# New SBUF places for an up projection's operands, w_out's weights split earlier and kept in DRAM, and new step orders

## The chip, the cores and the metric

The kernel runs on one core of a Trainium2 chip. The time is the device time of one execution in microseconds; that of several runs is given as their median. The engines: PE is TensorE, ACT is ScalarE, DVE is VectorE, POOL is GpSimd, and SP is the engine that issues nearly all DMA transfers here, one after the other in the order of its program. Every engine works its instructions off in program order and waits on semaphores for what others make.

## The reference

One step of one layer of a decoder, for a prompt of 2048 rows and a sample group of 8 sequences with 8 new rows each. D is 1024, the inner width 4096.

```python
h = rmsnorm(x, g_pre_mix)
proj = h @ w_in                                   # 1024 x 1280: q (512), k (128), v (128), u (512)
attn = sliding-window attention with rotary q, k and a sink per head   # window 128, 8 heads, 2 kv heads
pooled = per group: (mean of the last 2/4/8/16 rows of u - u) @ pool_w, times pool_scale
mix = concat(rmsnorm(attn, g_attn), rmsnorm(pooled, g_pool)) @ w_out
x = x + rmsnorm(mix, g_post_mix)
hf = rmsnorm(x, g_pre_mlp)
ff = square(relu(hf @ w_up)) @ w_down
x = x + rmsnorm(ff, g_post_mlp)
x = x + sigmoid(x @ w_ple_gate + b_ple_gate) * (pe @ w_ple)
```

Beside the two y, the outputs are the last 128 rows of k and v and the last 15 of u of each group. For the sample group most of these rows are those of the input states, shifted by 8 places: they are copied from DRAM to DRAM.

## The kernel before

**Arithmetic.** A product of 32-bit numbers is made of three passes with rounded halves: the high half (fp32r) times the high half, high times low and low times high. So every operand is "split": ScalarE casts or scales it into the high half (`split_into`, L195 to L197; for weights with a gain `A.mul`), VectorE subtracts that from the whole and gets the low half (`lo_of`, L127; for weights with a gain `scalar_tensor_tensor`, STT below).

**First stage (0 to about 452 us).** The sample rows are tile -1, the prompt's 16 tiles of 128 rows are 0 to 15. For each tile `head` loads x, its transposed copy xt and the rotary table cs; `front` makes q, k, v and u (products qps, kvps, ups with the split w_in, wi); `attention`, `pooling` and `finish` follow one tile behind, and `finish` stores the tile's mix to DRAM (mixd, L633). w_in is loaded in eight slices through a ring of four buffers (`load_w_in`, L322 to L327). The work of a tile is woven by hand-written strings (ORDER, L44): each letter takes one step of `a` attention, `p` pooling, `f` the next tile's front, `l` the last tile's finish, `e` extra work; ORDER1 and ORDER2 serve the last two tiles. A scheduler then orders the instructions of each engine from that, and may take DMAs without waits much earlier: the three state copies of L1100 to L1102 stand in the text in the up projection, but in SP's program in sixth to eighth place.

**w_out (452 to about 633 us).** In the last tile, as `e`, the class `Mixed` loads w_out raw in 8 units of two 128-row pieces by 512 columns, scales and splits them (`unit`, L210 to L227), and starts w_out's products (`product`, L240; tile of PSUM: pab). mr is a tile's mix read back, ms its split. After each tile come residual, second norm, and transposed h, stored to DRAM with its sums (hfd). The prompt's last two tiles' residual and turning are "late": they run in the up projection.

**Up projection (633 to about 1296 us).** The product hf @ w_up goes by a 7-product scheme in place of 8: the rows stand in three blocks, the columns in 16 pairs (`DFF // 256`). One `UpQuad` is a block and a pair j: seven products of 12 matmuls of 128x352, in the order p1, p2, p6, p7, p5, and `end` in the next round. Their left operands are the weights' seven combinations (raw -> g, differences at L984), their right ones seven operands of the block (loaded from hfd as sp, split into op; `load_ops`). In the first round two quads run side by side. `rest` (after p6 of that round) turns the second late tile, adds four op places, and loads operands five and six. `Ring` is a list of buffers that are used in turn; a pool's buffers lie where earlier pools lay, and a load into one waits until their last reader is done.

**Down projection, gate and the end (1296 to 2188 us).** Neither changes but for the state copies.

## Time and profile before

| | us |
|---|---|
| runs | 2188.45, 2188.64, 2188.88 (median 2188.64) |
| the profiled execution, its own time | 2190.07 |
| its span in the profile | 2188.3 |
| busy: PE / DVE / ACT / POOL | 2135.2 / 1591.6 / 958.8 / 568.5 |
| waits of PE that the trace names, the five longest groups | 7.5, 7.1, 6.0, 5.5, 4.3 |

The busy times overlap; an engine that is idle costs nothing unless the end waits for it. In a list of waits a row reads: engine, the waiting line, the releasing engine with its tile and line, then microseconds in total, number, and the longest. In a table of stretches a row reads: stretch, its length, then for each engine busy microseconds with the number of instructions, the clock that TensorE was granted (1.00 is full), the DMA engines' mean busy share, and GB/s. In a timeline: start, duration, engine, line, operation, and in brackets the idle time ahead of it with what ended it. A matmul at half clock counts as busy, so lost clock does not show as idle time.

### The profile page before, as it was taken

The page shows a single profiled execution, that of the slowest core. Times are in us where ns is not written, and L with a number is a line of the kernel's source. Part 1 is how long each engine was busy: PE and PEld are TensorE (multiplying, and loading weights), DVE is VectorE, ACT ScalarE, POOL GpSimd, SP SyncE. Part 2 cuts the span into 40 slices and gives each one's busy share as a digit, 9 for nine tenths or more (in the row PEclk, how much of TensorE's full clock was granted, in tenths as well). Part 3 has the DMA queues.
Part 4 walks back from the last instruction along what each step waited for, and adds up shares of the span by engine and source line. Part 5 has one row for each costly group of instructions (what it writes and reads, how often), then busy time and mean ns, then how long its engine had stood idle before and what let it go on. Part 6 is the DMA issues. An engine that isn't in the chain of part 4 may idle for free. (4 is left out here: it accounts for less than half of the span.)

```text
span 2188.3 us, 31100 instructions
## 1 busy us (share of the span) xinstructions
PE 2135.2 (98%) x11435; PEld 1884.1 (86%) x11435; DVE 1591.6 (73%) x2716; ACT 958.8 (44%) x1856; POOL 568.5 (26%) x642
## 2 busy tenths in 40 slices
PE   7999999889989999999999999999999999999999
PEld 5888888678878999999999988788888888888887
DVE  5788889866587777655755565888988888876553
ACT  4666666644465445444644454332232233232221
POOL 2334333233341000000000035535535535300000
PEclk9999999989999999999999999999999999999999
DMA  6212212457799768766676642222222221342211
GB/s 224 67 61 84 68 61 73 136 173 216 214 278 326 234 216 261 224 194 192 201 221 192 195 125 68 89 72 76 89 80 77 90 94 63 118 136 82 87 54 39
DMA packets 305985, 303.64 MB, mean 139 GB/s; under 512 B 78950, under 2 KB 257330, under 8 KB 299657
## 3 DMA queue, kind: packets, MB, share of 16 engines
q1 hardware_dynamic: 305833, 301.66, 44.1%
q8 instruction: 90, 1.47, 0.3%
q14 instruction: 62, 0.51, 0.1%
HBM read 208.78 MB, written 94.12 MB: 138 GB/s over the span
## 5 line engine op out<-in xcount | busy, mean ns | idle before, releaser
L1020 PE MATMUL up<-op,g 128*128 128x352 f32 x1344 | 433.6, 324 | 8.3 <-ACT snap L1027 7.5
L1021 PE MATMUL up<-op,g 128*128 128x352 f32 x1344 | 432.9, 322 | 5.5 <-DVE op L127 5.5
L1022 PE MATMUL up<-op,g 128*128 128x352 f32 x1344 | 421.8, 324 | 2.2 <-DVE g L127 2.2
L1247 DVE TENSOR_TENSOR z<-dn,z 128x512 f32<-128x512 f32 x416 | 277.2, 684 | 72.4 <-PE dn L1239 64.3
L127 DVE TENSOR_TENSOR g<-raw,g 128x512 fp32r<-128x512 f32 x336 | 229.0, 700 | 86.2 <-ACT g L197 85.8
L1020 PEld LDWEIGHTS up<-op,g 128*128 128x128 f32 x1344 | 252.7, 188 | 10.2 <-ACT snap L1027 8.6
L1021 PEld LDWEIGHTS up<-op,g 128*128 128x128 f32 x1344 | 254.2, 189 | 6.3 <-DVE op L127 6.1
L1022 PEld LDWEIGHTS up<-op,g 128*128 128x128 f32 x1344 | 251.2, 189 | 2.7 <-DVE g L127 2.7
L197 ACT CAST g<-raw 128x512 fp32r<-128x512 f32 x336 | 203.9, 623 | 104.5 <-PE up L1022 90.0
L1186 POOL TENSOR_TENSOR raws<-raws 128x1024 f32<-128x1024 f32 x32 | 84.4, 2647 | 619.1 <-DVE wr L127 424.1
L1237 PE MATMUL dn<-wr,ms 128*128 128x512 f32 x512 | 199.3, 390 | 0.8 <-DVE z L1247 0.8
L1238 PE MATMUL dn<-wr,ms 128*128 128x512 f32 x512 | 199.2, 389 | 0.0
L1239 PE MATMUL dn<-wr,ms 128*128 128x512 f32 x512 | 198.2, 389 | 0.0
L1034 DVE TENSOR_TENSOR t<-up,snap 128x352 f32<-128x352 f32 x144 | 71.1, 521 | 116.0 <-ACT snap L1027 99.8
L1237 PE MATMUL dn<-wr,m 128*128 128x512 f32 x384 | 149.5, 389 | 1.7 <-DVE z L1247 1.7
L1238 PE MATMUL dn<-wr,m 128*128 128x512 f32 x384 | 149.4, 389 | 0.0
L1239 PE MATMUL dn<-wr,m 128*128 128x512 f32 x384 | 149.1, 389 | 0.0
L197 ACT CAST m<-fr 128x512 fp32r<-128x512 f32 (+1 forms) x128 | 65.2, 513 | 188.5 <-PE dn L1239 166.6
L830 POOL TENSOR_TENSOR s<-fr 128x256 f32<-128x256 f32 x64 | 53.8, 840 | 321.4 <-DVE ms L127 222.0
L1027 ACT COPY snap<-up 128x352 f32<-128x352 f32 x144 | 61.1, 454 | 168.9 <-PE up L1022 168.8
L197 ACT CAST wr<-raws 128x1024 fp32r<-128x1024 f32 x66 | 69.1, 1051 | 119.2 <-PE dn L1239 57.8
L1237 PEld LDWEIGHTS dn<-wr,ms 128*128 128x128 f32 x512 | 96.1, 188 | 21.3 <-issue 1.2
(269 smaller groups left out, 4943.4 us busy)
## 6 DMA issues: line engine op xcount, KB each, us to landing
raw<-in_w_up_dram SPq DMA_DIRECT2D x160, 256.0 KB, 4.6
raw<-upt SPq DMA_DIRECT2D x32, 1024.0 KB, 7.8
fr<-ffd SPq DMA_DIRECT2D x64, 512.0 KB, 3.7
ffd<-r SPq DMA_DIRECT2D x96, 256.0 KB, 2.7
upt<-raw SPq DMA_DIRECT2D x16, 1024.0 KB, 4.0
raws<-in_w_down_dram SPq DMA_DIRECT2D x32, 512.0 KB, 5.0
sp<-hfd SPq DMA_DIRECT2D x21, 704.0 KB, 7.3
x<-in_x_prompt_dram SPq DMA_DIRECT2D x16, 512.0 KB, 4.5
```

The source lines that it names most:

```text
L127: eng.tensor_tensor(out=out, in0=full, in1=hi.bitcast(F32), op=ALU.subtract)
L197: copy(out=dst[:, 0], in_=src)
L1020: T.matmul(ps, l[0], r[0], start=st, stop=False, skip_group_check=not fresh)
L1021: T.matmul(ps, l[0], r[1], start=False, stop=False, skip_group_check=not fresh)
L1022: T.matmul(ps, l[1], r[0], start=False, stop=c == 3, skip_group_check=not fresh)
L1027: A.copy(out=s, in_=ps)
L1034: V.tensor_tensor(out=t, in0=ps, in1=s, op=ALU.add)
L1186: G.tensor_tensor(out=t, in0=x, in1=y, op=ALU.subtract)
L1237: T.matmul(ps, l[0], r[0], start=fresh and j == 0, stop=False, skip_group_check=not fresh)
L1238: T.matmul(ps, l[0], r[1], start=False, stop=False, skip_group_check=not fresh)
L1239: T.matmul(ps, l[1], r[0], start=False, stop=j == 1, skip_group_check=not fresh)
L1247: V.tensor_tensor(out=z, in0=ps, in1=z, op=ALU.add)
```

## The change

- **Start.** `load_gains` comes first, then xt of tile -1 and two slices of w_in, only then x and cs; the ring has six buffers. The state copies now are issued through `queue` (which keeps program order) in the down projection.
- **w_out.** `split_w_out` is the `e` of tiles 3 to 10: one unit a tile, two pieces of 128x512 each loaded, scaled, subtracted and stored to a DRAM tensor wod, with two raw buffers (wraw) and one for the split pieces (wsp). `unit` then only loads 1 MB of finished halves. Tiles 3 to 10 have their own string, ORDERW; ORDER1 and ORDER2 are new.
- **Up projection.** Each operand has a named place; the rings for weights, raw weights and operands lie otherwise, so that some no longer lie over what w_out's last products read. The first round is one quad. The late residuals and turnings are spread over the first two rounds, and in the third `space` makes room for two more operands' places and three of g.

```diff
+ORDERW = "e a e f f l f f f f p a f f f e f a f f p a f f f f p a a l"
-ORDER1 = "f a f f f l f f a f f a f p f f f f p l f a a p a"
-ORDER2 = "e a p l a p e l a p e a e a e e"
+ORDER1 = "f a f f f l a f f f p f a f f f f f p l f a a a p"
+ORDER2 = "e a p l a a e l a p e a e p e e"
...
+    wod = {(u, nh): dp.tile([P, 2, 2, 512], F32, name=f"wod{u}{nh}") for u in range(4) for nh in range(2)}
...
         def unit(self, u, nh):
-            ns = slice(nh * 512, nh * 512 + 512)
-            raw = self.mrp.tile([P, 2, 512], F32, tag="raw", bufs=4, name="raw")
-            if u >= 2:
-                SY.dma_start(raw, w_out[u * 256 : (u + 1) * 256, ns].rearrange("(k p) f -> p k f", p=P))
-            else:
...
             w = self.wo[nh * 4 + u].tile([P, 2, 2, 512], F32R, name="wo")
-            for k in range(2):
-                g = gout[:, 2 * u + k : 2 * u + k + 1]
-                A.mul(out=w[:, 0, k], in_=raw[:, k], mul=g)
-                V.scalar_tensor_tensor(
-                    out=w[:, 1, k], in0=raw[:, k], scalar=g, in1=w[:, 0, k].bitcast(F32), op0=ALU.mult, op1=ALU.subtract
-                )
+            SY.dma_start(w.bitcast(F32), wod[u, nh])
             self.w[u, nh] = w
...
         def load_w_in(k):
-            raw = over.pool.tile([P, INC], F32, tag="raw", bufs=4, name="raw")
+            raw = over.pool.tile([P, INC], F32, tag="raw", bufs=6, name="raw")
...
+            if t < 0:
+                queue(xt[:, :, :n], x_t[:, :, c0 : c0 + n])
+                for k in range(2):
+                    load_w_in(k)
             x = fp.tile([P, D], F32, tag="x", bufs=1, name="x")
             queue(x[:n], xrows(t))
...
+        def split_w_out(u, nh):
+            ns = slice(nh * 512, nh * 512 + 512)
+            raws = []
+            for c in (2 * u, 2 * u + 1):
+                raw = over.pool.tile([P, 512], F32, tag="wraw", bufs=2, name="wraw")
+                raws.append(raw)
+                if u >= 2:
+                    SY.dma_start(raw, w_out[c * P : (c + 1) * P, ns])
+                else:
+                    for g in range(2):
+                        SY.dma_start(raw[g * HD : g * HD + HD], w_out[g * 256 + c * HD : g * 256 + (c + 1) * HD, ns])
+            yield
+            for k, raw in enumerate(raws):
+                w = over.pool.tile([P, 2, 512], F32R, tag="wsp", bufs=1, name="wsp")
+                gain = gout[:, 2 * u + k : 2 * u + k + 1]
+                A.mul(out=w[:, 0], in_=raw, mul=gain)
+                V.scalar_tensor_tensor(
+                    out=w[:, 1], in0=raw, scalar=gain, in1=w[:, 0].bitcast(F32), op0=ALU.mult, op1=ALU.subtract
+                )
+                SY.dma_start(wod[u, nh][:, k], w.bitcast(F32))
+                yield
...
-                e = iter(())
+                e = split_w_out((t - 3) % 4, (t - 3) // 4) if 3 <= t < 11 else iter(())
...
-            ops = Ring(s3, "op", 5)
+            g3 = Ring(s3, "g3", 7)
+            sp_late = Ring(s3, "spl", 1)
+            ops = {n: Ring(s3, n, 1) for n in ("l0", "l1")}
             p3 = pool(s3, "p3")
+            raw3 = Ring(s3, "raw", 1)
             sp3 = Ring(s3, "sp", 1)
-            raw3 = pool(s3, "raw3")
-            sp3.more(1)
-            sp3.n = 1
-            g3 = Ring(s3, "g3", 10)
-            g3.n = 4
+            raw3.more(1)
+            raw3.n = 1
+            ops |= {n: Ring(s3, n, 1) for n in ("e3", "e4", "e0", "e1", "e2")}
...
+            PLACES = (
+                ("e0", "e1", "e2", "e3", "e4", "l0", "l1"),
+                ("x0", "x1", "e0", "e1", "e2", "l0", "l1"),
+                ("e3", "e4", "x0", "x1", "e0", "e1", "e2"),
+            )
...
+            def space():
+                operands(NT // 2 - 1, *late_h)
+                s2r.close()
+                for n in ("x0", "x1"):
+                    ops[n] = Ring(s3, n, 1)
+                g3.first(3)
...
-                rounds = [todo[:2]] + [[q] for q in todo[2:]]
+                rounds = [[q] for q in todo]
...
+                o7s[0] = load_ops(0, OPS[:5])
                 prepare(0)
-                o7s[0] = load_ops(0, OPS[:5])
-
-                def rest():
-                    turn_late()
-                    ops.more(4)
-                    o7s[0].update(load_ops(0, OPS[5:]))
+                sp3.slots.append(sp_late.slots[0])
+                sp3.n = 1
+                o7s[0].update(load_ops(0, OPS[5:]))
+
+                behind = {
+                    0: {"p6": lambda: residual_late(0), "p5": lambda: residual_late(1)},
+                    1: {"p6": turn_late, "p5": turn_late},
+                    2: {"p2": space},
+                }
...
+                        if g == 1 and tp == 3:
+                            queue(o["new_k_sample"][0, :, : WIN - TDEC], i["state_k"][0, :, TDEC:])
+                            queue(o["new_v_sample"][0, :, : WIN - TDEC], i["state_v"][0, :, TDEC:])
+                            queue(o["new_pool_sample"][0, :, : HALO - TDEC], i["state_pool"][0, :, TDEC:])
```

Three places show what the change does to the order of an engine's instructions. The first is VectorE in an early tile, from the scaling of the rotary table (cs) on; line numbers after the change are three higher there. Before:

```order
228 L364 TENSOR_SCALAR cs<-cs,rsq 128x128
229 L453 CAST kp<-kp 128x4x128
230 L611 CAST rr<-r 128x512
231 L397 TENSOR_TENSOR qr<-qps,cs 128x512
232 L400 TENSOR_TENSOR rb<-qps,cs 128x8x32 x2
233 L551 COPY part<-po 64x512
234 L127 TENSOR_TENSOR rr<-r,rr 128x512
235 L630 TENSOR_SCALAR ss_1472<-pss 128x2
236 L552 TENSOR_TENSOR mix<-po,part 64x512
237 L438 CAST qhl<-qr 128x8x64
```

After:

```order
230 L367 TENSOR_SCALAR cs<-cs,rsq 128x128
231 L400 TENSOR_TENSOR qr<-qps,cs 128x512
232 L130 TENSOR_TENSOR rr<-r,rr 128x512
233 L403 TENSOR_TENSOR rb<-qps,cs 128x8x32 x2
234 L130 TENSOR_TENSOR hT<-xt,hT 128x512 x2
235 L633 TENSOR_SCALAR ss_1480<-pss 128x2
236 L768 SCALAR_TENSOR_TENSOR wsp<-wraw,gains,wsp 128x512
237 L554 COPY part<-po 64x512
238 L441 CAST qhl<-qr 128x8x64
239 L555 TENSOR_TENSOR mix<-po,part 64x512
240 L130 TENSOR_TENSOR qhl<-qr,qhl 128x8x64
241 L768 SCALAR_TENSOR_TENSOR wsp<-wraw,gains,wsp 128x512
```

The 16 subtractions of w_out (wsp) now stand between the tile's own instructions. Though the strings give them to eight tiles, all 16 stand between six rows of cs: 2, 4, 4, 3 and 3 of them in five periods.

The second place is ScalarE in the last tile, where the softmax (pr) and its sums (es) stand. Before:

```order
343 L511 ACTIVATE pr,sm<-pr,nm 128x256
344 L540 CAST pt<-trp 128x512
345 L511 ACTIVATE pr,sm<-pr,nm 128x256 x3
346 L223 ACTIVATE wo<-raw,gains 128x512 x2
347 L511 ACTIVATE pr,sm<-pr,nm 128x256
348 L521 ACTIVATE es<-es 128x4
349 L223 ACTIVATE wo<-raw,gains 128x512 x2
350 L511 ACTIVATE pr,sm<-pr,nm 128x256 x3
351 L223 ACTIVATE wo<-raw,gains 128x512 x4
352 L521 ACTIVATE es<-es 128x4
353 L197 CAST ms<-mr 128x1024
```

After:

```order
341 L514 ACTIVATE pr,sm<-pr,nm 128x256
342 L543 CAST pt<-trp 128x512
343 L514 ACTIVATE pr,sm<-pr,nm 128x256 x4
344 L524 ACTIVATE es<-es 128x4
345 L580 COPY ux<-tru 128x4x128
346 L514 ACTIVATE pr,sm<-pr,nm 128x256 x3
347 L524 ACTIVATE es<-es 128x4
348 L529 ACTIVATE pr<-pr,es 128x256 x2
349 L558 ACTIVATE sq<-mix 128x512
350 L543 CAST pt<-trp 128x512
351 L529 ACTIVATE pr<-pr,es 128x256 x2
```

w_out's multiplications no longer stand between the softmax's rows. Its loads now are eight of 1 MB on SP, the first two ahead of the store of u's last rows, the others behind it, before and behind the first two mr.

The third place is SP at the end of w_out and the start of the up projection. Before, four of the first block's operand loads (sp) stand at the end of it, behind the first weights, with the next quads' weights between them:

```order
179 L964 DMA sp<-hfd_5421 128x1408
180 L996 DMA upt_5434<-raw 128x2048
181 L964 DMA sp<-hfd_5421 128x1408
182 L854 DMA xt<-in_x_prompt_dram 128x1024
183 L858 DMA x1d_5464<-xt 128x1024
184 L885 DMA hfd_5423<-h 128x4x128
185 L964 DMA sp<-hfd_5421 128x1408
186 L885 DMA hfd_5423<-s 128x16x128
187 L964 DMA sp<-hfd_5421 128x1408
188 L858 DMA x1d_5465<-xt 128x1024
189 L964 DMA sp<-hfd_5421 128x1408
190 L976 DMA raw<-in_w_up_dram 128x4x128 x4
```

After, they are spread among w_out's own transfers; of the stretch with six of the seven, this is a part:

```order
173 L996 DMA sp<-hfd_5489 128x1408
174 L884 DMA x1d_5524<-xt 128x1024
175 L880 DMA xt<-in_x_prompt_dram 128x1024
176 L230 DMA mr<-mixd_92 128x1024
177 L996 DMA sp<-hfd_5489 128x1408
178 L911 DMA hfd_5489<-h 128x4x96
179 L911 DMA hfd_5490<-h 128x4x32
180 L911 DMA hfd_5489<-s 128x16x96
181 L911 DMA hfd_5490<-s 128x16x32
182 L884 DMA x1d_5525<-xt 128x1024
183 L996 DMA sp<-hfd_5489 128x1408
184 L911 DMA hfd_5490<-h 128x8x128
```

The first quad's weights stand far ahead of these, in the last tile. The places of the sixth and seventh operand lie over w_out's weights; the load of the seventh and the second quad's weights follow at the end of w_out.

More of the change, by code (lines that the diff above doesn't have):

```diff
@@ L329, in load_pool_w @@
         def load_pool_w():
-            raw = over.pool.tile([P, INC], F32, tag="raw", bufs=4, name="raw")
+            raw = over.pool.tile([P, INC], F32, tag="raw", bufs=6, name="raw")
             pr = raw[:, 0:512].rearrange("p (g d) -> p g d", g=4)
@@ L914, in trunk @@
                         turn(due.pop(0))
-            normed |= {t: first_residual(t) for t in late}
             late_h = []
@@ L1106, in up_rounds @@
                     quads[-1].ahead = ahead
[L1107 to L1108 removed]
+                    quads[-1].then = behind.get(k, {})
                     yield quads
```

42 lines of the change are left out of this document (19 added, 23 removed).

## The prediction

> **What bounds the kernel now.** I read the chain of waits first, then TensorE's waits, then busy time by stage.
>
> ```profile
> PE 39%; DVE 1%; DMA 0%; POOL 0%; issue 0%; ACT 0%; SPq 0%; POOLq 0%
> ```
> ```profile
> PE up L1020 <- ACT snap L1027: 7.5, 4, 3.0
> PE trp L538 <- DVE pr L528: 7.1, 1, 7.1
> PE gps L298 <- DMA graw<-in_g_pre_mix_dram: 6.0, 1, 6.0
> PE up L1021 <- DVE op L127: 5.5, 2, 3.5
> PE pss L628 <- POOL sq L624: 4.3, 1, 4.3
> PE kvps L131 <- ACT wi L326: 4.1, 2, 2.8
> ```
> ```profile
> core 0: us, PE busy (x) PEld busy (x) DVE busy (x) ACT busy (x) POOL busy (x), PEclk, DMA share, GB/s
> 0.00:30.00 30.00, 18.88 (x76) 11.65 (x77) 15.06 (x18) 16.51 (x19) 3.12 (x17) 0.94 0.93 314
> 126.00:149.00 23.00, 23.00 (x147) 20.12 (x146) 20.30 (x57) 14.81 (x39) 9.35 (x12) 1.00 0.23 73
> 149.00:173.00 24.00, 24.00 (x151) 21.15 (x150) 20.86 (x60) 14.29 (x38) 9.66 (x11) 1.00 0.23 69
> 389.00:402.00 13.00, 5.54 (x38) 4.41 (x37) 12.22 (x35) 11.11 (x31) 0.72 (x2) 0.81 0.88 258
> 397.00:408.00 11.00, 4.93 (x16) 0.53 1.05 323
> 402.00:452.00 50.00, 42.13 (x213) 34.62 (x214) 39.20 (x81) 30.24 (x65) 16.88 (x18) 0.88 0.35 111
> 441.00:445.00 4.00, 4.00 (x19) 0.57 0.38 131
> 448.00:459.00 11.00, 7.22 (x20) 0.53 0.68 240
> 500.00:560.00 60.00, 60.00 (x286) 49.77 (x285) 35.53 (x33) 29.34 (x51) 24.14 (x35) 1.00 0.77 217
> 633.00:680.00 47.00, 34.22 (x186) 31.82 (x187) 39.82 (x44) 25.87 (x43) 16.97 (x14) 0.89 0.94 300
> 680.00:720.00 40.00, 40.00 (x253) 40.00 (x252) 32.91 (x56) 20.86 (x39) 0.00 (x0) 1.00 1.02 325
> 1290.00:1300.00 10.00, 7.04 (x38) 1.00 0.69 195
> ```
>
> The chain ends on TensorE. Its products are the same in both kernels, so a gain can only come from its idle time and from time at a half clock. The rows put both in three places: the start (30.00 − 18.88 = 11.1 us idle), the last tile (7.46 + 7.87 = 15.3 idle at 389 to 452, and matmuls busy 4.93 + 4.00 + 7.22 us at a clock near 0.55, of which half, 8.1, is lost: 23.4), and the start of the up projection. There 186 matmuls take 47 us; at the next row's 40.00 / 253 = 0.158 us they would take 29.4: 17.6 lost, 12.8 of them idle. A middle tile (126 to 173) leaves TensorE no idle time at all.
>
> **The start.** ScalarE's rows, an SP row, and one of the page.
>
> ```profile
> 12.30 1.36 ACT L326 ACTIVATE wi<-raw,gains 128x1280 fp32r<-128x1280 f32 x1 [0.18 <-DMA raw<-in_w_in_dram]
> 18.95 1.36 ACT L326 ACTIVATE wi<-raw,gains 128x1280 fp32r<-128x1280 f32 x1 [5.29 <-DMA raw<-in_w_in_dram]
> 20.53 1.36 ACT L326 ACTIVATE wi<-raw,gains 128x1280 fp32r<-128x1280 f32 x1 [0.23 <-DMA raw<-in_w_in_dram]
> 5.26 0.76 SPq L1100 DMA_DIRECT2D out_new_k_sample_dram<-in_state_k_dram  x1
> DMA  6212212457799768766676642222222221342211
> ```
>
> ScalarE scales one w_in slice per landing. Slices land 1.58 us apart, but 6.65 lie between the fourth and the fifth, because the three state copies (the first issued at 5.26) stand between them on SP and four buffers hold the ring. The change moves the copies to the down projection and gives the ring six buffers: 6.65 − 1.58 = 5.1 us off the fifth landing. The gains and two slices now come ahead of x (about 1 us sooner); x's sum of squares is wanted only behind the products. TensorE then becomes the bound: it starts cold, and the 4.1 us that it waits for wi are the surest part of the gain. I take **−4.3**, those and little more; bounds −3 (cold products eat a part) and −6.1 (5.1 + 1). The last row is the page's DMA share in 40 slices of 55 us: in the down projection (slice 25 on) it is 0.2 to 0.4, so the copies cost 0 there, at most +2 if a weight pair lands late.
>
> **w_out's split in tiles 3 to 10.**
>
> ```profile
> L223 ACT ACTIVATE wo<-raw,gains x16: 706/712/729, 394.8 to 413.3; 128x512 fp32r<-128x512 f32 x16
> L224 DVE SCALAR_TENSOR_TENSOR wo<-raw,gains,wo x16: 740/747/753, 395.6 to 414.8; 128x512 fp32r<-128x512 f32 x16
> mixd<-mix SPq DMA_DIRECT2D x2, 512.0 KB, 2.6
> SPq L633 <- DVE mix L552: 124.0, 6, 23.5
> ```
>
> The same 16 multiplications (16 × 0.71 = 11.4 us of ScalarE) and 16 subtractions (16 × 0.75 = 12.0 of VectorE) move here from the last tile. By the program's order they fall into five tile periods, 2, 4, 4, 3 and 3 of them: four bring VectorE from 20.3 of 23 us to 23.3, and from 20.86 of 24 to 23.9. It is full there, and TensorE, which had no idle time, waits for every other VectorE wait that remains. Also one buffer holds a split half, so the next multiplication waits for the store before it: 0.71 + 0.75 + an issue of some 0.35 + 2.6 (the same 512 KB as a mixd store) = 4.4 us from one to the next. ScalarE is in order; behind a multiplication that waits stand qT, pt and the softmax rows, and for those TensorE waits. On SP, x, xt and cs of the next tile stand behind these stores and behind the mixd store, which already waits up to 23.5 us. The order leaves mostly 7 to 13 ScalarE instructions between two multiplications, enough for 4.4 us, but 4 to 6 in four cases. Bounds: below, −2 (looser new step order, since x may come sooner); above, four short gaps at 2 us and 1 us in each of the two full periods, +10, and 2 more for SP. I take **+4**.
>
> **The last two tiles.**
>
> ```profile
> 394.84 1.33 ACT L223 ACTIVATE wo<-raw,gains 128x512 fp32r<-128x512 f32 x2 [0.75 <-DMA raw<-in_w_out_dram]
> 397.38 1.33 ACT L223 ACTIVATE wo<-raw,gains 128x512 fp32r<-128x512 f32 x2 [0.62 <-DMA raw<-in_w_out_dram]
> 400.10 2.54 ACT L223 ACTIVATE wo<-raw,gains 128x512 fp32r<-128x512 f32 x4
> 402.55 0.19 ACT L521 ACTIVATE es<-es 128x4 f32<-128x4 f32 x1
> 402.00 0.66 PE L538 MATMUL trp<-ident,pr 128*128 128x128 f32 x2 [7.13 <-DVE pr L528]
> 451.77 1.02 PE L628 MATMUL pss<-small,sq 128*128 128x1 f32 x4 [4.31 <-POOL sq L624]
> ```
>
> The 7.13 us stall is ScalarE's and VectorE's w_out work, some of it waiting for raw w_out, in line ahead of es and pr of the same tile; 5.2 us of multiplications lie in the rows. After the change ScalarE goes from es to the next softmax rows directly, so this wait goes whole, unless es itself is late. A new wait can come in: eight 1 MB loads replace 4 MB of raw weights. At the start a 640 KB slice lands every 1.58 us, 415 GB/s, so 8 MB take 20 us; w_out's first column half (4 MB) and two 512 KB mr tiles need 12.7. The first two loads wait only for w_in's last readers, the third stands behind the pool-state store that waits for u (389 in before), so the first products can start near 402 to 404, as now. TensorE reaches that point with some 4.5 us of other products done more. The 4.31 us wait for POOL's sq stays in its cause, but two dozen of w_out's products (24 × 60.00 / 286 = 5.0 us) now stand ahead of it. I leave 5 us of idle and 3 us of half clock: 23.4 − 8 = **−15**; bounds −21 (2 left) and −8 (the 7.13 gone, nothing else).
>
> The clock: behind the 7.13 us wait follow some 10 us at 0.53, behind the 4.31 as many. But a row at 0.57 (441 to 445) follows no long wait, while 2.96 us without work at 1290 to 1300 (the 3.0 for snap in the list) left the clock at 1.00. The Trainium skill, "TensorE: Matmul & The Clock Gate", section "Part 1: The HAM clock gate", has the clock halved after an idle window of some 3.4 us that runs freely. The trace agrees for the long waits and not for 441. By that rule waits under 3.4 us would leave no half clock: the last tile would be −18, not −15.
>
> **The up projection's places.**
>
> ```profile
> 635.55 0.42 PE L1020 MATMUL up<-op,g 128*128 128x352 f32 x1 [2.81 <-ACT snap L1027]
> 639.51 0.66 PE L1021 MATMUL up<-op,g 128*128 128x352 f32 x1 [3.54 <-DVE op L127]
> L197 ACT CAST op<-sp 128x1408 fp32r<-128x1408 f32 x8 | 10.8, 1370 | 0.6 <-DMA sp<-hfd 0.6
> L127 DVE TENSOR_TENSOR op<-sp,op 128x1408 fp32r<-128x1408 f32 x7 | 12.3, 1775 | 2.8 <-ACT op L197 2.8
> sp<-hfd SPq DMA_DIRECT2D x7, 704.0 KB, 4.6
> ```
>
> Seven operands of the first block are loaded, cast and split; before, one or two of them by the end of w_out, the others between the products that wait for them. Now five stand in the attention's freed area, split during w_out, with quad 0's weights, and the first round is one quad instead of two. The five cost ScalarE 5 × 1.37 and VectorE 5 × 1.78 = 8.9 us earlier; the row at 500 to 560 shows VectorE 35.53 of 60, ScalarE 29.34: hidden, **+0.5** (0 to +3 if POOL's chain in w_out is met). If that cover were gone it would be 8.9. So the waits for op (5.5) and most of those for snap go. Late next: quad 1's weights. Their buffer's load stands on SP behind an operand's load that waits for its buffer; DMA share is 0.94 and 1.02, and 1 MB of weights plus two operands (2.4 MB at 300 GB/s, 8 us) must land within quad 0 (84 × 0.158 = 13.3 us) and be split behind the operands: some 2 us of wait, 2 us of snap behind casts in ScalarE's line, 2 us of half clock. 17.6 − 6 = **−12**; bounds −16 and −4 (transfers still the pace).
>
> **The sum**: −4.3 + 4 − 15 − 12 + 0.5 = −26.8. The profiled execution took 2190.07 us, its span 2188.3, the runs' median 2188.64 (1.4 under it, 0.07%, and I carry the difference unchanged): **2162 us**. Half-widths of the terms (2, 6, 6, 6) joined as independent give about ±11: its own range 2151 to 2174.
>
> **Rivals.**
> - *No half clock left* between 389 and 680, by the rule above: the 3 and 2 us I keep go too, 2157. For it: my remaining waits are all short. Against: the row at 441. Chance 0.12.
> - *The up start stays with the transfers*: share 0.94 to 1.02 in 633 to 720 does not fall, only arrives otherwise; that term −4, 2170. Against: five operands' 3.5 MB move into w_out, where the share is 0.77. Chance 0.14.
> - *The split bites*: +14 instead of +4, from VectorE full in its periods, 2172. Chance 0.14.
> - *The last tile keeps its wait* because the wo loads (8 MB for 4) come too late in place of the arithmetic: −4 there, 2173. Against: they can start earlier than the raw ones. Chance 0.05.
> - *Slower*: the store loop. Multiplication, subtraction, store and next multiplication hold ScalarE, the stores hold x behind them on SP. The other terms sum to −30.8; 16 halves turn that round from 1.9 us lost in each, of the 4.4 that a loop has. At 2.3 each: 2195. For it: 23.5 us waits on SP and a full VectorE. Against: share 0.23, and 24 us tiles into which 3 to 4 loops fall. Chance 0.10, half of it beyond +0.2%.
> - The forecast: 0.45.
>
> The bound of what can be told from no change is 0.2%, 4.4 us. Faster 0.90, the same 0.05, slower 0.05. The range 2146 to 2179 takes in the rivals on the fast side.
>
> **What would show it.** Right: in 0 to 30 no step over 2 us between wi rows; in the last tile no wait of TensorE for pr over 1 us; no wait for op at the up start, and 41 us or more of TensorE busy in its first 47. Wrong: TensorE below 23.5 of 24 us in tiles 3 to 8 with ScalarE waiting for a wod store; a long wait of pab for wo; a wait for g in the second quad over 4 us. A period over 28 us in five tiles would bring the whole forecast down.

## The result

The changed kernel takes 2170.93 us (median of four runs, 2167.38 to 2173.31) against 2188.55: ratio 0.9921, 95% interval 0.9905 to 0.9936. Measured once more beside the experiments it took 2167.32 (2166.66 to 2171.18) against 2188.93: ratio 0.9902, 0.9887 to 0.9916. So it is 18 to 22 us faster; 26.8 less, 2162, was forecast, with a range that holds both medians. The profiled execution took 2167.38 us, the fastest of its four, and its span is 2165.6. It stands 22.7 under the profiled one of before; the ledger below is that of these two.

### The profile after

The waits of TensorE in the changed kernel (columns as before):

```profile
PE kvps L134 <- ACT wi L324: 5.2, 1, 5.2
PE up L1060 <- ACT snap L1067: 5.0, 2, 4.1
PE trp L541 <- DVE pr L531: 3.9, 1, 3.9
PE pab L134 <- ACT z L252: 3.5, 4, 1.8
PE dn L1276 <- DVE z L1286: 3.1, 2, 1.7
PE gps L296 <- DMA graw<-in_g_pre_mix_dram: 2.3, 1, 2.3
PE trk L453 <- DVE pt L130: 2.2, 1, 2.2
PE trp L541 <- ACT vp L426: 1.7, 1, 1.7
PE trx L896 <- DVE ez L886: 1.5, 1, 1.5
PE ups L134 <- DVE es L525: 1.2, 1, 1.2
PE pss L631 <- POOL sq L627: 0.8, 1, 0.8
```

Against the list of before: the wait for pr has gone from 7.1 to 3.9, that for POOL's sq from 4.3 to 0.8, the 5.5 for op is gone. New are the evictions of w_out (z, 3.5 us in four), the turning (trx) and two waits in the early tiles (vp, es). The wait for wi has not gone: it is 5.2 us in one, ahead of the first product, where it was 4.1 in two. Stretches of the changed kernel (columns as in the prediction's table of stretches):

```profile
0.00:30.00 30.00, 21.94 (x103) 14.70 (x104) 18.96 (x27) 17.31 (x19) 5.55 (x18) 1.00 0.99 305
126.00:150.00 24.00, 21.08 (x129) 18.10 (x128) 21.08 (x56) 16.62 (x42) 10.57 (x13) 1.00 0.61 200
389.00:397.00 8.00, 1.92 (x11) 1.56 (x11) 7.81 (x21) 5.11 (x15) 5.24 (x6) 0.76 1.02 421
397.00:437.00 40.00, 39.24 (x207) 33.63 (x206) 29.55 (x64) 22.11 (x47) 9.78 (x12) 0.92 0.50 185
480.00:560.00 80.00, 76.74 (x365) 62.92 (x364) 51.17 (x45) 38.46 (x61) 32.18 (x42) 1.00 0.81 238
620.00:670.00 50.00, 45.82 (x276) 45.14 (x275) 46.17 (x62) 27.48 (x50) 14.48 (x12) 0.93 0.92 293
```

One middle tile now has 2.9 us of idle TensorE (126 to 150) where there was none, w_out has 3.3 in 80 us, and the start of the up projection is busy 45.82 of 50 us, where it was 34.22 of 47. The DMA share there is as high as before.

### Where the time went

Idle time leaves out lost clock, so I made a ledger of lost time: the time between two points of the program, less the matmuls between them at their usual pace. The pace is the median distance of two starts of a kind in the kernel before (0.227 us for 128x512, 0.160 for 128x352). The points: the q transposes of tiles 3, 9 and 14, the last pss product, w_out's 769th product, the up projection's 337th. The names of the stretches are those of the expectations. What is called tiles 3 to 10 ends with the q transposes of tile 9 (267.9 us in the changed kernel, behind all 16 of w_out's multiplications); in pinned five of the 16, in inplp and best four, lie behind that point. The first column is the time of the first q transpose. "Faster" is the median against the kernel before on the same chip; the interval is in the text where a verdict needs it.

| kernel | first q transpose | tiles 3-10 | tiles 11-15 | last tile | w_out | up start | faster |
|---|---|---|---|---|---|---|---|
| before | 37.3 | 1.1 | 6.7 | 22.7 | 2.8 | 18.5 | |
| **changed** | 33.1 | 5.8 | 0.2 | 12.1 | 7.5 | 7.4 | 17.6 |
| changed, second profile | 33.3 | 8.1 | 0.2 | 11.4 | 5.4 | 8.2 | 21.6 |
| nostt | 32.6 | 13.3 | 0.7 | 10.8 | 1.0 | 7.3 | 22.5 |
| pinned | 35.4 | 4.5 | 4.4 | 17.6 | 2.8 | 7.3 | 18.3 |
| lateops | 33.2 | 6.5 | 0.2 | 12.4 | 6.1 | 28.5 | 0.0 |
| nosplit | 32.5 | 0.6 | 0.5 | 8.4 | 0.7 | 7.9 | 35.2 |
| xtf | 31.6 | 7.0 | 0.2 | 12.4 | 4.5 | 7.2 | 21.8 |
| old12 | 33.0 | 9.9 | 0.2 | 19.2 | 3.9 | 6.9 | 14.0 |
| csb (on before) | 36.9 | 1.0 | 0.3 | 29.5 | 2.5 | 20.0 | -3.6 |
| mrb | 32.2 | 7.6 | 0.2 | 11.5 | 2.6 | 7.8 | 25.2 |
| inplp | 33.2 | 2.5 | 2.9 | 11.5 | 2.2 | 6.7 | 26.3 |
| copies (on before) | 34.3 | 0.9 | 6.4 | 22.5 | 2.0 | 17.6 | 2.6 |
| best | 32.9 | 2.6 | 1.9 | 11.2 | 0.4 | 6.4 | 31.3 |

The change itself: start -4.1, tiles 3 to 10 +4.7, tiles 11 to 15 -6.5, last tile -10.6, w_out +4.7, up start -11.1: -22.9; everything behind the up start stays within 1.

### The profile page after: what moved, and what is told of

Read it like the earlier page. It is cut to its first block, busy times and chain, and to the rows that moved or that the text cites. A ratio compares the mean times of both kernels' runs of the same rounds, so it can differ in the third digit from the quotient of the medians.

```text
span 2165.6 us, 31185 instructions
## 1 busy us (share of the span) xinstructions
PE 2127.1 (98%) x11435; PEld 1879.0 (87%) x11435; DVE 1581.1 (73%) x2716; ACT 958.5 (44%) x1856; POOL 566.7 (26%) x642
## 4 chain that ended last, share of the span: by engine, by line
PE 81%; DVE 7%; DMA 4%; issue 3%; POOL 3%; ACT 2%; SPq 1%; POOLq 0%; ACTq 0%; DVEq 0%
PE up L1060 9%; PE up L1062 9%; PE up L1061 9%; PE dn L1276 9%; PE dn L1278 9%; PE dn L1277 9%; PE pg L136 3%; PE pg L135 3%; PE pg L134 3%; PE ups L134 1%; PE ups L136 1%; PE ups L135 1%; PE qps L135 1%; PE qps L134 1%; PE qps L136 1%
## 5 line engine op out<-in xcount | busy, mean ns | idle before, releaser
L1060 PE MATMUL up<-e,g 128*128 128x352 f32 x832 | 269.8, 325 | 5.1 <-ACT snap L1067 5.0
L1061 PE MATMUL up<-e,g 128*128 128x352 f32 x832 | 268.3, 322 | 0.0
L1062 PE MATMUL up<-e,g 128*128 128x352 f32 x832 | 264.5, 324 | 0.0
L1060 PEld LDWEIGHTS up<-e,g 128*128 128x128 f32 x832 | 157.0, 189 | 6.1 <-ACT snap L1067 5.6
L1061 PEld LDWEIGHTS up<-e,g 128*128 128x128 f32 x832 | 157.8, 190 | 0.1
L1062 PEld LDWEIGHTS up<-e,g 128*128 128x128 f32 x832 | 156.0, 189 | 0.0
L1276 PEld LDWEIGHTS dn<-wr,ms 128*128 128x128 f32 x512 | 96.1, 188 | 21.8 <-issue 1.8
```

Of the source, the lines that this page charges most:

```text
L1060: T.matmul(ps, l[0], r[0], start=st, stop=False, skip_group_check=not fresh)
L1061: T.matmul(ps, l[0], r[1], start=False, stop=False, skip_group_check=not fresh)
L1062: T.matmul(ps, l[1], r[0], start=False, stop=c == 3, skip_group_check=not fresh)
L1276: T.matmul(ps, l[0], r[0], start=fresh and j == 0, stop=False, skip_group_check=not fresh)
```

## The experiments

### The same kernel again

> The changed kernel once more, nothing edited. It shows how far its executions lie apart (2167.4 to 2173.3 so far, the profiled one the fastest) and which stage carries the spread. Lost time means: time between two points of the program less the matmuls between them at their usual pace; in the profiled run after the change: tiles 3 to 10 5.8, tiles 11 to 15 0.2, last tile 12.1, w_out 7.5, start of the up projection 7.4. Theory A (the spread comes from the loop of w_out's store, whose length varies with the transfers): tiles 3 to 10 lose 5 to 12 this time, all else within 1 us. Theory B (it comes from the start of the up projection, where the transfers are full): tiles 3 to 10 within 1 of 5.8, up start 7 to 13. Median 2168 to 2173 by either.

The median is 2167.32. Tiles 3 to 10 lose 8.1 this time, w_out 2.1 less, the last tile 0.6 less, the up start 0.8 more. So the early tiles do vary, as theory A had it (ScalarE waits 9.1 us for stores instead of 8.2), but not they alone, and the end did not move: the span is 2165.4 against 2165.6. What the tiles lose more, w_out loses less. From two profiles that is only a sign, the first one, that w_out waits for something besides TensorE. The kernel before, too, lay between 2185.1 and 2192.0 on this chip, so a spread of some 6 us is nothing of the change's own.

### The split: VectorE, or the loop through the store

The subtraction left out (nostt), and the 16 multiplications pinned into more tile periods (pinned):

```diff
-                A.mul(out=w[:, 0], in_=raw, mul=gain)
-                V.scalar_tensor_tensor(...)
+                A.mul(out=w, in_=raw.unsqueeze(1).to_broadcast([P, 2, 512]), mul=gain)      # nostt
...
-                A.mul(out=w[:, 0], in_=raw, mul=gain)
+                tc.keep_in_program_order(A.mul(out=w[:, 0], in_=raw, mul=gain))             # pinned
```

> Leaves out w_out's subtraction in tiles 3 to 10: ScalarE writes both halves in one multiplication of 128x1024 (1.1 us instead of 0.71), VectorE does nothing for w_out; loads, stores and the single buffer stay. Theory A (VectorE, full in these periods, carries the cost): tiles 3 to 10 lose 1 to 2 us instead of 5.8, total 4 to 5 us faster than the changed kernel, near 2166. Theory B (the loop through the store: the next multiplication waits in ScalarE's line until the last store has landed): the loop is as long as before (1.1 + 0.35 + 2.9 against 0.7 + 0.75 + 0.35 + 2.9), ScalarE still waits some 8 us for stores, and the stage still loses 4 us or more: total within 2 us of the changed kernel.

> Each of w_out's 16 multiplications is pinned behind the instruction traced before it on ScalarE, so that they spread over nine tile periods (1 to 3 in each) instead of five. Theory B (loop through the store): two multiplications stand 10 us or more apart, ScalarE waits under 2 us for stores, and tiles 3 to 10 lose 1 to 2 us: 4 us faster than the changed kernel, near 2166. Theory A (VectorE full): 1.5 to 2.25 us per period fit into its 3 us of idle time: as much faster. A third theory, that any new instruction in these in-order lines costs its place: no gain, 5 us or more lost, now over nine periods.

Without any work for w_out on VectorE the tiles lose 13.3 us, more than with it: the loss does not need a full VectorE. Some 4.6 of the 13.3 are lost clock, which the changed kernel has none of there: the granted clock in nostt is 0.57 in 145 to 149 and in 203 to 211, with 3.25 and 7.37 us of TensorE busy. Two rows of the timeline of the changed kernel, one of ScalarE's waits at 100 to 260, and four of the chain of work that ended last show the loop:

```profile
130.85 0.72 ACT L767 ACTIVATE wsp<-wraw,gains 128x512 fp32r<-128x512 f32 x1 [2.08 <-DMA wod<-wsp]
131.61 0.75 DVE L768 SCALAR_TENSOR_TENSOR wsp<-wraw,gains,wsp 128x512 fp32r<-128x512 f32 x1 [1.69 <-ACT wsp L767]
```
```profile
ACT wsp L767 <- DMA wod<-wsp: 8.2, 7, 2.1
```
```profile
118.94 4.55 DMA wod<-wsp
127.58 3.17 DMA wod<-wsp
130.85 0.73 ACT wsp L767
143.31 1.22 DVE pr L531 x2
```

The multiplication stands at the head of ScalarE's line for 2.08 us until the store before it has landed, and VectorE's subtraction waits 1.69 for it. From there the chain goes through the lines of VectorE and ScalarE to TensorE's product at 146.48, ahead of which TensorE stood still for 1.66 (trp for vp) and 1.24 us (ups for es). So in this period the loop lies on the path that sets the time.

It is not the whole price. In pinned no multiplication waits for a store any more, yet 4.5 us are lost in tiles 3 to 10, and 4.4 in 11 to 15, where nothing was lost: 8.9 together, against 6.0 and 8.3 in the two profiles of the changed kernel. TensorE's waits there are short ones, none over 0.8 us. Its last tile was laid out otherwise and lost 17.6, 5.2 of it waiting for POOL's sq. Of the three theories for pinned, the third held: no gain, and 5 us or more lost.

The whole price of the split:

```diff
-                e = split_w_out((t - 3) % 4, (t - 3) // 4) if 3 <= t < 11 else iter(())
+                e = split_w_out(0, 0) if t == 3 else iter(())
...
-            SY.dma_start(w.bitcast(F32), wod[u, nh])
+            SY.dma_start(w.bitcast(F32), wod[0, 0])
```

> Leaves out w_out's scaling and splitting but for one of its eight units; all eight 1 MB loads then read that one unit, so loads and their sizes stay. Theory A (the split is what tiles 3 to 10 lose more than before): they lose 1 to 2 us instead of 5.8 to 8.1, and everything behind them comes 5 us sooner, total 2161 to 2163. Theory B (the end of w_out hangs on another chain than TensorE's and stands near 608.3, where it stood in three kernels): tiles lose as little, but w_out loses 10 or more, and the total stays at 2166 to 2168.

It is faster than before by 35.2 us (ratio 0.9841, 0.9827 to 0.9856), 13.6 more than the changed kernel was by its second measurement, where 5 were expected. Tiles 3 to 10 lose 0.6: that part is the split's. But w_out also loses 0.7 instead of 5.4 to 7.5, and the last tile 8.4 instead of 11.4 to 12.1, though it still loads 8 MB (one unit, eight times). The program's order there is another one, and for w_out that was followed up; why the last tile loses less was not.

### w_out: what the first residual waits for

Operands 1, 3 and 5 of the first block behind w_out (lateops):

```diff
-                o7s[0] = load_ops(0, OPS[:5])
-                prepare(0)
-                sp3.slots.append(sp_late.slots[0])
+                sp3.slots.insert(0, sp_late.slots[0])
+                o7s[0] = load_ops(0, OPS[:5])
+                prepare(0)
```

> Operands 1, 3 and 5 of the first block go through the buffer that lies over w_out's weights, so they are loaded and split only behind w_out's last products; operands 2 and 4 stay early. Theory A (w_out lost 4.7 us more because ScalarE's casts of these operands wait for their loads ahead of w_out's evictions): w_out loses 4 to 5 us instead of 7.5. Theory B (w_out loses that for its own order, turning the first tiles sooner): 7 or more as now. By both, the start of the up projection loses 14 to 20 instead of 7.4, since the first product waits for a 7 us load, a cast and a subtraction: total 2176 to 2183.

w_out loses 6.1, between the 7.5 and 5.4 of the two profiles with all five: the casts of the operands are not what costs there (and in best, below, all five stand in w_out, which loses 0.4). The up start is another matter: 28.5 us, 20 more than with early operands, and the whole kernel is back at the time of before (ratio 1.0001, 0.9992 to 1.0010). TensorE's longest waits at 608 to 702 in this kernel:

```profile
PE up L1060 <- ACT e L207: 13.0, 2, 8.4
```

Three operands that come late cost 13.0 us for casts alone, the longest 8.4. So the early operands are what the layout's gain at the up start rests on, though the kernel before, with other places and two quads in its first round, lost less (18.5) than this one.

Four of the six gaps that TensorE has in w_out lie ahead of the first cast of an operand (524.41). VectorE's waits and SP's issues at the end of the last tile of the changed kernel:

```profile
DVE ez L882 <- DMA g_post_mix<-in_g_post_mix_dram: 6.1, 1, 6.1
DVE xt L883 <- DMA xt<-in_x_prompt_dram: 2.8, 1, 2.8
```
```profile
432.82 0.56 SPq L636 DMA_DIRECT2D mixd<-mix  x1
437.47 0.32 SPq L230 DMA_DIRECT2D mr<-mixd  x1
437.84 0.42 SPq L178 DMA_DIRECT2D g_post_mix<-in_g_post_mix_dram  x1
438.32 0.42 SPq L178 DMA_DIRECT2D g_pre_mlp<-in_g_pre_mlp_dram  x1
438.79 0.90 SPq L880 DMA_DIRECT2D xt<-in_x_prompt_dram  x2
```
```profile
447.67 1.24 DVE xt L883
451.03 1.30 DVE ez L886
452.37 1.09 PE trx L896 x8
```

The last three rows are from the chain of waits in that stretch. The first residual needs the post-mix gains and x. Both stand on SP behind one mr load, which goes at 437.47, when VectorE has finished with the buffer before it. x lands at 447.5, the first turn runs at 452.37, and TensorE had to wait 1.5 us for it, and again behind it. Before, the same loads went at 449.4 to 452, while TensorE itself stood still until 451.77 for POOL's sq: that wait had hidden them.

Across the kernels the loss in w_out follows the moment of the first x load against the end of the last pss product: 2.3 us behind it 5.4 to 7.5 are lost (changed, twice; lateops 6.1), 1.9 behind 4.5 (xtf), 0.6 behind 3.9 (old12); 0.8 to 1.5 ahead of it 0.7 to 2.8 (before, nostt, pinned, csb, nosplit). In nosplit they go so:

```profile
424.36 0.64 SPq L178 DMA_DIRECT2D g_post_mix<-in_g_post_mix_dram  x1
425.10 0.38 SPq L178 DMA_DIRECT2D g_pre_mlp<-in_g_pre_mlp_dram  x1
425.57 0.85 SPq L880 DMA_DIRECT2D xt<-in_x_prompt_dram  x2
429.13 0.33 SPq L230 DMA_DIRECT2D mr<-mixd  x1
```

with the mr load behind them. Two edits try the order itself, x ahead of the pre-MLP gains (xtf), and with it that mr load behind both x loads (mrb):

```diff
-            gpost, gmlp = rows_of(p2, "g_post_mix"), rows_of(p2, "g_pre_mlp")
+            queue(gpost, i["g_post_mix"].to_broadcast([P, D]))
+            queue(xt0[0], xrows(0))
+            queue(gmlp, i["g_pre_mlp"].to_broadcast([P, D]))
...
             SY.dma_start(raw[:, :, :n], mixd[t])      # in load(t); mrb: for t == 4 ordered behind the load of x of tile 1
```

> The first x rows of w_out's residuals are loaded ahead of the pre-MLP gains instead of behind them; nothing else is edited. Theory A (w_out starts late because VectorE waits 6.1 us for the post-mix gains and then 2.8 for x, and the first turn waits for that): x lands about 2 us sooner, the wait of the first turn (0.9 to 1.5 us) goes, w_out loses 4 to 5.5 us instead of 5.4 to 7.5, total 1 to 2 us faster. Theory B (TensorE's own order makes the stalls): w_out within 1 us of 5.4 to 7.5, total unchanged within 1.

> In the changed kernel SP issues the residual's first loads (post-mix gains, x) behind one mr load that waits for VectorE. Here that mr load stands behind them, and x ahead of the pre-MLP gains. Theory A (w_out's loss follows the moment of these loads: in eleven profiles, where the first x load goes 1.9 to 2.3 us behind the end of the last pss product w_out loses 4.5 to 7.5, at 0.6 it loses 3.9, at -0.8 to -1.5 it loses 0.7 to 2.8): the loads go 3 us or more sooner, w_out loses 1 to 3.5 us, total 2161 to 2165. Theory B (TensorE's order and ScalarE's casts of the operands make the stalls): w_out loses 4.5 or more, total within 2 of the kernel with x first (2165.4).

xtf alone loses 4.5 in w_out, as theory A had it, but the first turn still waits 1.0 us, and the total (21.8 faster) is that of the changed kernel (21.6): too small to tell. With the mr load moved too, the gains go at 433.76 instead of 437.84:

```profile
433.76 0.42 SPq L127 DMA_DIRECT2D g_post_mix<-in_g_post_mix_dram  x1
437.43 0.33 SPq L127 DMA_DIRECT2D xt<-in_x_prompt_dram  x1
438.77 0.43 SPq L230 DMA_DIRECT2D mr<-mixd  x1
```

x itself goes only 1.4 us sooner than in the changed kernel (438.79), less than the 3 that were expected. w_out loses 2.6, all gaps ahead of 520 are gone, and the kernel is 25.2 us faster than before (ratio 0.9887, 0.9871 to 0.9903). Theory A holds for w_out and for the total. (The profiled execution, 2166.32, was the slowest of the four; it lost 3 us to a half clock at 1386 to 1393, behind the stretches of the table.)

### The last tile: arithmetic or order

old12 is the changed kernel with ORDER1 and ORDER2 as they were.

> The changed kernel with the step orders that the last two tiles had before. Theory A (what the last tile gains comes from w_out's arithmetic having left the lines of ScalarE and VectorE): the last tile loses 11 to 14 us, as with the new orders (11.4, 12.1), total within 2 of 2167. Theory B (it comes from the new orders): 17 to 22, near the 22.7 of before, total 2173 to 2178.

The last tile loses 19.2, theory B's number, and the kernel is 14.0 us faster than before instead of 21.6 (ratio 0.9933, 0.9916 to 0.9950). TensorE's waits there, with the old orders:

```profile
PE pss L631 <- POOL sq L627: 7.1, 2, 6.2
PE trp L541 <- DVE pr L531: 3.1, 1, 3.1
```

The wait for pr is short as soon as w_out's arithmetic is gone (3.1, against 7.1 before), but without the new orders the wait for sq grows to 6.2. Moving the arithmetic is worth some 3.5 us of the last tile (22.7 to 19.2), the orders on top of it another 7; the new orders without the moved arithmetic were not tried.

### Tiles 11 to 15, where nothing had been forecast

VectorE's timeline in one of these tiles, before and in the changed kernel:

```profile
316.72 0.29 DVE L364 TENSOR_SCALAR cs<-cs,rsq 128x128 f32<-128x128 f32 x1 [1.72 <-POOL rsq L140]
316.92 1.28 DVE L127 TENSOR_TENSOR hT<-xt,hT 128x512 fp32r<-128x512 f32 x2
```
```profile
312.35 1.30 DVE L130 TENSOR_TENSOR hT<-xt,hT 128x512 fp32r<-128x512 f32 x2 [0.39 <-ACT hT L376]
313.56 0.28 DVE L367 TENSOR_SCALAR cs<-cs,rsq 128x128 f32<-128x128 f32 x1
```

Before, the scaling of cs stands ahead of the split of hT and waits for POOL, and hT, which TensorE waits for, comes behind it. In the changed kernel hT stands first here and in the tile before, and half of it in the next. The same order was made in the kernel before (csb):

```diff
-            V.tensor_scalar_mul(cs[:n], cs[:n], rs[:n])           # in head(t); now only for t < 9
...
+            if t >= 9:                                             # in split_head(t), behind hT
+                tc.keep_in_program_order(V.tensor_scalar_mul(cs[:n], cs[:n], rs[:n]))
```

> The kernel before with one edit: in tiles 9 to 15 VectorE scales the rotary table (cs, which waits for POOL's rsq) behind the split of the transposed x (hT) instead of ahead of it, the order that the changed kernel happens to have there. Theory A (that order is what tiles 11 to 15 gained in the changed kernel, 6.5 us): they lose 0.2 to 1.5 us instead of 6.7, total 5 to 6 us faster than before, 2182 to 2184. Theory B (VectorE is busy 21.1 to 21.5 of 24 us there, and any other order stalls elsewhere): 5 or more lost, total within 2 of before.

VectorE's longest wait in these tiles, before, changed, and in csb:

```profile
DVE cs L364 <- POOL rsq L140: 8.6, 5, 1.7
```
```profile
DVE cs L367 <- POOL rsq L143: 2.2, 2, 1.7
```
```profile
DVE cs L377 <- POOL rsq L140: 0.9, 2, 0.4
```

The tiles lose 0.3 us instead of 6.7: the mechanism is right. The total is not: 2190.76 against 2187.19, ratio 1.0015 (1.0006 to 1.0025). The scheduler laid the last tile out otherwise, and there two waits for POOL's sq stand where there was one:

```profile
PE pss L631 <- POOL sq L627: 8.7, 2, 4.4
PE trp L541 <- DVE pr L531: 7.7, 1, 7.7
```

The last tile ends at 452.7, as in the kernel before (452.8). So a stall that goes is worth nothing if the next stage is laid out to end at the same time.

### The start

copies is the kernel before with the three state copies in the down projection.

> The kernel before with one edit: the three state copies are issued in the down projection. Theory A (they alone make the start's gain, 4.1 us): the fifth slice of w_in lands 4 to 5 us sooner, all tiles come 3.5 to 4.5 us sooner, total 2183 to 2185. Theory B (the order of the first loads and the six buffers make most of it): 1 to 2 us only, total 2186 or more. The down projection loses nothing by both.

All tiles come 2.9 us sooner, between the two theories; the median is 2.6 us lower (ratio 0.9985, 0.9975 to 0.9994). The longest step between two slices of w_in falls from 6.65 to 3.1 us (15.34 to 18.42). The copies had not held the fifth slice's load on SP: it goes at 10.61 in the kernel before and at 10.52 here, in both behind 3.0 us of waiting for VectorE to have read a buffer of the ring. What they held was its transfer: ScalarE takes the slice at 18.95 before, at 15.34 here. Why 3.1 us still lie between the fifth and the sixth, whose load goes at 12.21, stays open. The other 1.2 us of the changed kernel's 4.1 come from the order and the ring, not tried apart; its first product starts 1.2 us sooner (7.81 instead of 9.05).

### A kernel that is faster than both

inplp splits w_out in place, with two buffers for each half, and pins each multiplication; best adds csb's edit. Both contain mrb.

```diff
-                w = over.pool.tile([P, 2, 512], F32R, tag="wsp", bufs=1, name="wsp")
+                w = over.pool.tile([P, 512], F32R, tag="wsp", bufs=2, name="wsp")
...
+                tc.keep_in_program_order(A.mul(out=w, in_=raw, mul=gain))
+                lo = raw.bitcast(F32R)
+                V.scalar_tensor_tensor(out=lo, in0=raw, scalar=gain, in1=w.bitcast(F32), op0=ALU.mult, op1=ALU.subtract)
+                SY.dma_start(wod[u, nh][:, k, 1], raw)
+                SY.dma_start(wod[u, nh][:, k, 0], w.bitcast(F32))
```

> The kernel with the moved mr load, and w_out's split made in place: two buffers for the raw piece, in which the low half then stands, two for the high half, each stored by itself; and each multiplication pinned behind the instruction traced before it on ScalarE: two pieces in each of eight tile periods, as the step order says. Same bytes, same 16 multiplications and subtractions. Theory A (the loop through the one buffer's store costs the tiles): ScalarE waits under 2 us for stores, tiles 3 to 10 lose 1 to 2.5 us instead of 5.8 to 8, total 3 to 6 us below the kernel with the moved mr load. Theory B (the sixteen additions to full in-order lines cost, wherever they stand): 4 us or more lost in tiles 3 to 15 together, total no better than 2 below it.

> The kernel with the in-place split and the moved mr load, and in tiles 9 to 15 the scaling of cs behind the split of hT on VectorE, as was tried in the kernel before; the order of the last tile stays as it is without this edit. Theory A (behind cs's wait for rsq the split of hT comes late; given back in the kernel before only because its last tile was laid out differently): tiles 11 to 15 lose 0.2 to 0.8 us instead of 2.9, the last tile 11 to 12 as now, total 2157 to 2160. Theory B (what tiles win there the last tile loses in any layout): last tile 13 or more, total 2160 to 2163.

In inplp no multiplication waits for a store any more, and this tile period is full of TensorE again:

```profile
124.00:148.00 24.00, 24.00 (x144) 21.00 (x144) 22.58 (x59) 15.74 (x41) 10.04 (x13) 1.00 0.41 123
```

Tiles 3 to 10 lose 2.5 instead of 7.6, as theory A had it. But four of the multiplications now stand in tiles 11 to 15, and these lose 2.9 instead of 0.2. Together that is 5.4 instead of 7.8, above the 4 of theory B, and the total is only 1.1 us further down than mrb's (26.3 against 25.2 faster), as theory B had it too. So with the loop's waits gone these tiles gain 2.4 us. With nearly all of the split left out they lose 1.1 (nosplit); the 4.3 between stay though no multiplication waits for a store. Which of the short waits carries them was not tried apart, and inplp differs from pinned in its places as well as in its buffers, so the share of the loop alone stays open. With cs behind hT these tiles lose 1.9, less of a gain than expected, the last tile 11.2, w_out 0.4:

```profile
437.00:600.00 163.00, 163.00 (x776) 134.81 (x775) 109.69 (x102) 84.45 (x139) 68.29 (x85) 1.00 0.77 231
```

best takes 2157.60 us against 2188.91 (ratio 0.9868, 0.9850 to 0.9887), the fastest of those that leave nothing out: against the kernel before it gains 10 us more than the changed kernel's better measurement.

## Why the prediction was right, and where it was not

The direction and the range held, and four of the sum's five terms lay inside their bounds.

- **The start** (-4.3): -4.1 measured. The reason given, the copies, carries 2.9 of it, by their transfers and not by their place on SP. The waits for wi, which were to be the surest part, were read wrongly: 2.81 of the 4.1 us stood ahead of the first product, and there 5.2 stand now, since the gains land sooner. What went are the 1.26 us between two slices, 0.80 for the low half behind it, and the lost clock that followed (0 to 30: 0.94 before, 1.00 after).
- **The split** (+4, up to +12): +4.7 and +7.0 in two profiles. The loop that was described is there: ScalarE waits 8.2 to 9.1 us for stores in seven to nine places. One loop took 7.0 us (123.84 to 130.85) where 4.4 were reckoned, 3.2 of them for the landing and 2.3 because the subtraction stood behind other work in VectorE's line. But pinned and inplp, without these waits, still lose 8.9 and 5.4 in tiles 3 to 15: the size was right for reasons of which the loop is one. The other reason given, a VectorE that is full, is not needed for the loss (nostt).
- **The last two tiles** (-15): -10.6. The failed sentence is that the 7.13 us wait "goes whole, unless es itself is late". es was late: without w_out's work the softmax's own chain still takes 3.9 us, and TensorE has nothing else, since w_out's first product comes at 403.5 (402 to 404 was forecast). And the half clock, of which I kept 3 us, stayed for 10 us behind it, some 4.0 (busy 1.76, 3.00 and 4.00 us at 0.53, 0.50 and 0.57 in the rows under "The clock"). The wait for sq went as forecast, for the reason given; old12 shows that this was the work of the new orders.
- **The up start** (-12): -11.1. No wait for operands is left; what remains is one for snap, 4.1 us, where 2 were expected. In ScalarE's line snap stands not only behind a cast but behind the late residual's sum of squares, which waited 5.1 us for VectorE's xt.
- **w_out** (+0.5, up to +3): +4.7 and +2.6. This is the step that failed. I asked whether the five operands' work is hidden, found busy shares that leave room, and it is hidden. I did not ask what else had run under the 4.3 us wait for sq that I let go: the residual's first loads. With that wait gone they are late, behind an mr load on SP. It is the question "where a stall goes, what is late next", put to TensorE's next product but not to the next stage's loads.
- **Tiles 11 to 15** (not forecast): -6.5, by luck of the order of cs and hT; without it the profiled gain would be 16.2 of the 26.8 that were forecast. The 2.8 us for hT stood in the list of waits of before; with the slower matmuls around them they were 6.7 of lost time, and I had looked only at tiles 126 to 173.

Added up, the missed terms are +4.4 (last tile), +4.2 (w_out), +0.7 (split), +0.9 (up start), +0.2 (start) and -6.5 (tiles 11 to 15): the profiled execution is 3.9 us off its forecast. The rest of the 9 us to the median of 2170.93 is that the profiled run of before was 1.4 above its median and this one 3.5 below. Of the rivals, "the split bites" was in the right place but at a third to half of its price, and the slower one did not come near: 8 us of waits in sixteen halves, where 1.9 in each would have been needed.

Of the signs that were named for right, two came (no wait for op, and TensorE busy at the up start) and two did not: ScalarE's wi rows still have steps of 3.2 and 2.9 us (6.39, 9.56, 12.49), and the wait for pr is 3.9 us, not under 1. Of those for wrong one came: TensorE is busy 21.08 of 24 us at 126 to 150, with ScalarE waiting for a wod store. The time held all the same, since that cost was in the sum.

**The clock.** Stretches of the changed kernel, for TensorE alone (the clock is the number ahead of the last two):

```profile
393.00:397.00 4.00, 1.76 (x11) 0.53 1.02 429
397.00:400.00 3.00, 3.00 (x15) 0.50 1.00 421
400.00:404.00 4.00, 4.00 (x21) 0.57 1.04 383
404.00:437.00 33.00, 32.24 (x174) 1.00 0.39 140
627.00:631.00 4.00, 3.86 (x13) 0.50 1.05 414
```

The granted clock drops to half at 393.2, behind the 3.94 us wait of the last tile, and at 625.3, 2.3 us after the 4.08 us wait at the up start began. The rule of the Trainium skill ("TensorE: Matmul & The Clock Gate", section "Part 1: The HAM clock gate"), a half clock behind an idle window of some 3.4 us, agrees with the length of both waits, though not with the moment of the second drop. In this kernel no shorter wait left a drop by itself; in others of this case some did: the clock is 0.57 at 203 to 211 in nostt, behind waits of 2.31 and 0.63 us, 0.57 at 147 to 151 in old12, behind 1.65 and 1.24 (the changed kernel has the same two waits, 1.66 and 1.24, and no drop), and 0.66 at 666 to 671 in the kernel before, behind 0.98, 1.17 and 1.20. The rival built on the rule did not come true: two waits of that length remained, and short waits close together can end in a half clock too.

## What to carry to other kernels

A stall is also the time in which the next stage's loads run: before letting one go, list what is issued during it, and move the loads that then come first ahead of any load on that queue that waits for an engine. A store through a single buffer puts its landing time at the head of an in-order engine's line; two smaller buffers in the same space took that wait away here, and with it 2.4 of the 7.8 us lost in tiles 3 to 15. A wait that is gone is not yet a gain: pinned lost its waits for stores too, and won nothing. And with a scheduler in between, a gain in one stage counts only after the order of the next has been looked at again: csb won 6.4 us in its tiles and lost 6.8 in the last one.

## What was not expected of the hardware

A store of 512 KB landed in 2.6 us in the kernel before (median), and that went into the loop's 4.4 us. In the early tiles of the changed kernel the same size took 2.9 (median), 3.17 and 4.55 in the chain above, and ScalarE's multiplication behind it could wait 2.2 us (again): a median says little about a loop that a landing time closes. And the up start runs with the DMA engines at a share of 0.92 (620 to 670; 0.94 at 633 to 680 before), yet loses 11 us less: a full share by itself did not set the loss there. What the order of the transfers is worth lateops shows: with three operands late the same stage loses 20 us more.
